# One layer of a hybrid encoder on one core: two projection tiles made together, one more set of weight sums made ahead, and the last product order of the last unit

## The chip, the cores and the metric

The kernel runs on one core of one Trainium2 chip. It is a single launch with no host arithmetic. The metric is the device time of the launch in microseconds (us), taken as the median of several runs. Five engines work side by side, each with its own instruction queue that runs in order: PE (matrix products; PEld is its weight load), DVE (elementwise work), ACT (elementwise functions and casts), POOL, and SP, which here does little but issue DMA transfers. An instruction waits at the head of its queue for semaphores, and what stands behind it waits with it.

## The reference, cut to what matters

```python
xn = RMSNorm(x);  y = xn @ W_in                       # 512 tokens x 2048, 59 column tiles of 128
h  = x + concat[GDN(y_gdn), RWKV7(y_rwkv)] @ W_out    # chunked recurrences of 64 tokens
h += CrossAttn(RMSNorm(h), RMSNorm(mem))              # 4 heads into 256 memory tokens (wk: keys)
u  = relu(RMSNorm(h) @ W_up) ** 2                     # 2048 -> 8192
h += u @ W_down                                       # 8192 -> 2048
out = RMSNorm_final(h)
```

All arrays are float32. Products are made from a high and a low part of each weight: `hi` is the weight rounded to the format that PE reads, `lo = w - hi`, and the products with both are added in PSUM.

## The kernel before

**Order of the work.** Every stage is written as Python generators that yield single operations. The planner `run` keeps a clock for each engine and, at each turn, issues the operation that could start first (a rank breaks ties). The result is a fixed order in each engine's queue; the clocks are the planner's own, so an order can be planned for times that the chip then does not keep. Changing one generator therefore also moves instructions of other generators that are in flight at the same time.

**Input projection.** For each of the 59 tiles `py0` to `py58`, two weight halves of 128x1024 are loaded (512 KB each) into a ring of three raw buffers `wraw`. ACT casts `whi<-wraw`, DVE makes `wlo<-wraw,whi`; these pairs form a ring of three as well. `gemm_` then issues three products for each of 16 row blocks (`xhi*whi`, `xlo*whi`, `xhi*wlo`), and DVE evicts the tile (`y<-py,rstd`). `gemm_` can work on several tiles at once: then it takes a half of each and goes through the row blocks once, tile by tile; the first two tiles are made that way. Between these products the recurrences of the heads are fitted in (`pkk`, `ri7x`, `ri7w`, `ri7s`, `ri7t`, `ri7u`, `pov` and so on are small PE products of the last head; `gk`, `k`, `r`, `E` are their operands, made by DVE; POOL makes an inverse that SP carries through DRAM as `bg16T`, `bg16U`). Around the last two tiles the memory tokens are loaded through the same raw ring (`wraw<-in_memT`) and become `mhl0` to `mhl15`, in the space that the blocks of x leave. After the projection come the keys: `kp0`, `kp1` and so on, from halves of `wk`.

**Down.** `u @ W_down` is done with seven products instead of eight for each pair of blocks. A unit of Down, such as (2,1), covers a quarter of the inner dimension (first number, `e`) and one of two column halves (second number, `m`). Its seven products are named B11, B21, T2, T1, T3, B22, T4 and use these weights: B11 takes the block A11, B21 takes A12, T4 takes A22, and the other four take sums of blocks: s1 = A21 + A22, s2 = s1 - A11, s3 = A11 - A21, s4 = A12 - s2. In most units the sums were made ahead: `presum` uses free moments of earlier stages to load columns of the four blocks, make the sums on DVE and store them to DRAM (`Sd`, in the trace `sd_s`). A unit then loads 28 halves of 512 KB, 4 for each product. For (3,0) and (3,1) the list `INSITU` says otherwise: each is split into two units, (3,0,(0,)), (3,0,(1,)), (3,1,(0,)) and (3,1,(1,)), called (3,0,0) to (3,1,1) below, and the sums are made by DVE in the loaded buffers themselves (`insitu`, two halves x of 128x1024 each). Such a unit has 14 halves, loads 8, and one of its products takes half as long as one of a full unit.

Each product writes two PSUM banks, for two blocks of 128 tokens: `mxd`, `mmd`, `mgd` or `scrd`, `scgd`. B11, T2, T3 and T4 share one pair of banks and add up in it, T1 and B22 another; B21 has its own. After each product DVE adds the bank to a row of the result, `h<-h,scrd` (a "snap"), and the next product in the same bank waits for that. The first and second 128 tokens (tokens 0 and 1 below) are complete after T4, tokens 2 and 3 after B22. When all four column blocks of a token block are complete, `final` takes the squares (ACT), and `store` makes the norm, scales by ACT (two column blocks) and DVE (two), and writes out 4 transfers of 256 KB, two from ACT's queue and two from SP's.

**Buffers at the end.** `wfree` holds the raw buffers (6, and 4 more, the tiles `ab` and `ws`, once the activations of Down are all cut), `hfree` the three hi/lo pairs. `loads` takes raw buffers in order; `splits` takes pairs in the order of the products.

Of the kernel before, what the change touches and what calls it, by code (L numbers as in the profile page):

```python
# [17 lines left out]
P = 128  # L18
# [55 lines left out]
def build(tc, I, out):  # L74
# [301 lines left out]
    mem4 = [I["memT"][:, k4 * 4:k4 * 4 + 4, :] for k4 in range(4)]  # L376
    NSQ = (50, 51, 52, 53)
    wq = [("w", I["w_in"][n][:, h * 1024:(h + 1) * 1024]) for h in range(2) for n in range(2)]
    for n in range(2, NIN):
        wq += [("s", mem4[j]) for j in range(4) if n == NSQ[j]]  # L380
        wq += [("w", I["w_in"][n][:, h * 1024:(h + 1) * 1024]) for h in range(2)]
    kpo = [(0, 0), (1, 0), (0, 1), (1, 1)] + [(n, h) for n in range(2, KD) for h in range(2)]
    INSITU = ((3, 0), (3, 1))
    GROUPS = [(e, m) for e in range(8) for m in range(2) if (e // 2, m) not in INSITU]
    A11, A21, A22, A12 = range(4)
    Sd = {(e, m, j): pd.tile([P, 2048], F32, name=f"sd{e}_{m}_{j}", tag=f"sd{e}_{m}_{j}")
          for e, m in GROUPS for j in ("s1", "s2", "s3", "s4")}
# [177 lines left out]
    def projections():  # L565
        pts = [psb(f"py{n}") for n in range(2)]
        yield from gemm_(pts, xhi, xlo, 0)
        for n in range(2):
            chain(evict(n, pts[n]), 0)
        for n in range(2, NIN):  # L570
# [10 lines left out]
            yield from gemm_([pt], xhi, xlo, 2 * n, left="x" if n == NIN - 1 else None)  # L581
            chain(evict(n, pt), 0)
        yield after("py", NIN - 2)
        kpt = {}
        for i, (n, h) in enumerate(kpo):
            if h == 0:
                yield after("kp", n - 2) if n >= 2 else after("py", NIN - 1)
                kpt[n] = psb(f"kp{n}", "mm", 2)
            pt = kpt[n]
            yield half(NKP + i)  # L590
            wh, wl = halves[NKP + i]
            for k in range(8 * h, 8 * h + 8):
                yield lambda: len(mhl) > k
                yield TE.matmul(pt, wh[:, k % 8 * P:k % 8 * P + P], mhl[k], start=k == 0, stop=False)
            for k in range(8 * h, 8 * h + 8):
                yield TE.matmul(pt[:, 0:M], wl[:, k % 8 * P:k % 8 * P + P], mhl[k][:, 0:M], start=False, stop=k == KD - 1)
            used.add(NKP + i)
            if h == 0:
                continue
            t = act_tile(f"khl{n}")  # L600
            khl.append(t)
            chain(kevict(n, pt, t[:, 0:M], t[:, M:2 * M]), 0)
        for i in range(2 * KD):
            n, g = i // 2, i % 2
            if i == 0:
# [1171 lines left out]
    def loads():  # L1777
        for u in units:
            kind, e, m = u[:3]
            if kind == "u":  # L1780
                src = I["w_up"][e]
                for i in (A11, A12, A22, A21) if u == units[0] else (A11, A21, A22, A12):
                    raws[u, i] = r = yield from take(wfree)
                    yield SY.dma_start(r, src[i])
                    events.add(("raw", u, i))
                continue
            if (e, m) in INSITU:
                for ws in (A11,), (A12,), (A21, "s1", A22):
                    for x in xs(u):
                        f, z = 2 * e + x // 2, x % 2  # L1790
                        for w in ws:
                            raws[u, w, x] = r = yield from take(wfree)
                            if w != "s1":
                                yield SY.dma_start(r, I["w_dm"][f, m, w][:, z * 1024:z * 1024 + 1024])
                                events.add(("raw", u, w, x))
                continue
            for i, w in order_of(u):
                for x in range(4):
# [5 lines left out]
                    events.add(("raw", u, i, x))  # L1804

    def ready(*keys):
# [43 lines left out]

    def insitu():
        for u in units:
            if u[0] != "d" or u[1:3] not in INSITU:
                continue
            for x in xs(u):
                yield lambda: all(("raw", u, w, x) in events for w in (A11, A21, A22))
                a11, a21, a22, s1 = (raws[u, w, x] for w in (A11, A21, A22, "s1"))
                yield tt(s1, a21, a22)
                events.add(("sum", u, "s1", x))
                yield tt(a21, a11, a21, ALU.subtract)  # L1860
                events.add(("sum", u, "s3", x))
                yield after("half", u, B11, x)
                yield tt(a11, s1, a11, ALU.subtract)
                events.add(("sum", u, "s2", x))
            for x in xs(u):
                yield after("half", u, B21, x)
                a11, a12 = (raws[u, w, x] for w in (A11, A12))
                yield tt(a12, a12, a11, ALU.subtract)
                events.add(("sum", u, "s4", x))
                yield after("half", u, T2, x)  # L1870
                wfree.append(a11)

    def splits():
        for u in units:
            if u[0] == "d" and u[1:3] in INSITU:
                for i, w in order_of(u):
                    for x in xs(u):
                        yield (after("sum", u, w, x) if isinstance(w, str) else after("raw", u, w, x))
                        r = raws[u, {"s2": A11, "s3": A21, "s4": A12}.get(w, w), x]
# [3 lines left out]
                        if w not in (A11, A12, "s2"):  # L1883
                            wfree.append(r)
                continue
            if u[0] == "d":
                for i, w in order_of(u):
                    for x in range(4):
# [219 lines left out]
    def downout(u, t, tag):  # L2108
# [6 lines left out]

        (x, kx) = banks_of[u, tag, t]
        mul = lambda i: after("mul", u, i, t)
        for i, tg, m, half, end in ((B11, tag, 0, 0, 0), (B21, "mm", 0, 0, 1), (T2, tag, 0, 1, 0), (T1, "mg", 1, 1, 0),
                                    (T3, tag, 1, 1, 0), (B22, "mg", 0, 1, 1), (T4, tag, 1, 0, 1)):
            yield mul(i)  # L2120
            b, kb = banks_of[u, tg, t]
            yield add(m, half, b)
# [136 lines left out]
    def finals():  # L2259
        yield lambda: acts_done and len(abfree) == 8  # L2260
        wfree.extend(abtiles + sfree_)
        yield after("spare7")
        wf.extend((hp[7][:, 0], hp[7][:, 1]))
        for _ in range(2):
# [132 lines left out]
```

## Time and profile before

| | us |
|---|---|
| median of 3 runs | 2909.23 |
| lowest and highest | 2908.71, 2913.34 |
| the profiled execution | 2912.32 |
| its span in the profile | 2910.4 |
| PE busy | 2872.1 |
| PE without work, all together | 38.3 |

The span runs from the first to the last recorded instruction or transfer; 1.9 us of the profiled execution lie outside it. PE is busy for nearly all of the span, so the time that a change can win is in the gaps of PE and at both ends; a row of the waits view gives how long an engine stood and what released it. In a timeline row the columns are start, duration, engine, line, operation, output and inputs, how many are merged in the row, and in brackets the idle time before it. In a row of the windows view stand the stretch, its length, the busy time of each engine, the clock that PE was granted (1.00 is full), the share of the DMA engines in use and what they moved.

### The profile page before, as it was taken

The numbers are of one execution on the slowest core, as the hardware profiler recorded it, in microseconds if no ns is written. First come the engines' busy times: TensorE is split into PE (matmuls) and PEld (weight loads), VectorE is DVE, ScalarE is ACT, GpSimd is POOL, SyncE is SP. The second block draws the span as 40 slices with busy tenths as digits, with TensorE's granted clock in tenths as the row PEclk, the third lists the DMA queues.
The fourth block names the chain that finished last, engine by engine and source line by source line (L and its number), as shares of the span: only waits on it lengthen the run. The fifth ranks groups of instructions, "written<-read, shape, count | busy, mean of one in ns | idle before, by whom it ended". The sixth has DMA issues, their size and how long they took to land.

```text
span 2910.4 us, 49156 instructions
## 1 busy us (share of the span) xinstructions
PE 2872.1 (99%) x18794; PEld 2421.0 (83%) x18794; DVE 2330.0 (80%) x3539; ACT 1569.2 (54%) x2233; POOL 224.8 (8%) x547
## 2 busy tenths in 40 slices
PE   8999999999999999999999999999999999999998
PEld 7887877777877888879988888888888888888786
DVE  7787787787887877769956898899998878776997
ACT  6454555555655555664445556555555644454544
POOL 0213213223213000000000000000000000000000
PEclk9999999999999999999999999999999999999999
DMA  5646656556666788784322354565556878876633
GB/s 190 177 140 181 165 156 171 167 153 180 179 168 188 219 255 274 230 286 152 125 95 88 108 167 156 192 202 193 184 195 193 290 225 283 259 236 207 198 109 105
DMA packets 314300, 541.47 MB, mean 186 GB/s; under 512 B 100360, under 2 KB 185612, under 8 KB 314064
## 3 DMA queue, kind: packets, MB, share of 16 engines
q1 hardware_dynamic: 286672, 506.87, 56.5%
q10 hardware_dynamic: 27392, 31.46, 3.1%
q8 instruction: 147, 2.41, 0.3%
q14 instruction: 89, 0.73, 0.1%
HBM read 436.11 MB, written 102.12 MB: 185 GB/s over the span
## 4 chain that ended last, share of the span: by engine, by line
PE 92%; DMA 3%; DVE 2%; ACT 1%; issue 1%; ACTq 0%; SPq 0%; DVEq 0%
PE py L256 22%; PE mxu L256 12%; PE mgu L256 6%; PE mgd L256 6%; PE mxd L256 6%; PE op L122 5%; PE vp L122 3%; PE sc L122 3%; PE at L122 3%; PE kp L256 3%; PE mmu L256 3%; PE scgd L256 3%; PE scrd L256 3%; PE mmd L256 3%; PE kq L256 3%; DMA wraw<-in_wo 1%
## 5 line engine op out<-in xcount | busy, mean ns | idle before, releaser
L256 ACT CAST whi<-wraw 128x1024 fp32r<-128x1024 f32 (+1 forms) x364 | 381.4, 1049 | 395.8 <-PE py L256 148.7
L256 DVE TENSOR_TENSOR wlo<-wraw,whi 128x1024 fp32r<-128x1024 f32 (+1 forms) x364 | 448.3, 1232 | 104.8 <-ACT whi L256 96.5
L256 PE MATMUL py<-xhi,whi 128*128 128x512 f32 x928 | 372.3, 401 | 7.9 <-ACT xhi L256 7.9
L256 PE MATMUL py<-xlo,whi 128*128 128x512 f32 x928 | 373.8, 403 | 0.0
L256 PE MATMUL py<-xhi,wlo 128*128 128x512 f32 x928 | 373.1, 402 | 0.0
L256 ACT CAST whi<-w 128x1024 fp32r<-128x1024 f32 x181 | 190.4, 1053 | 221.4 <-PE mxu L256 48.3
L256 DVE TENSOR_TENSOR wlo<-w,whi 128x1024 fp32r<-128x1024 f32 x181 | 220.9, 1222 | 54.1 <-ACT whi L256 52.0
L256 PE MATMUL mxu<-cb,whi 128*128 128x512 f32 x1016 | 255.0, 393 | 0.0
L256 PEld LDWEIGHTS py<-xhi,whi 128*128 128x128 f32 x928 | 175.1, 189 | 42.0 <-ACT xhi L256 7.9
L256 PEld LDWEIGHTS mxu<-cb,whi 128*128 128x128 f32 x1016 | 182.9, 189 | 32.6
L256 PEld LDWEIGHTS py<-xhi,wlo 128*128 128x128 f32 x928 | 175.2, 189 | 35.2 <-issue 1.8
L256 PEld LDWEIGHTS py<-xlo,whi 128*128 128x128 f32 x928 | 175.1, 189 | 35.1 <-DVE xlo L256 0.5
L131 DVE TENSOR_TENSOR wlo<-wraw,whi 128x1024 fp32r<-128x1024 f32 x112 | 136.8, 1223 | 44.9 <-ACT whi L130 44.0
L130 ACT CAST whi<-wraw 128x1024 fp32r<-128x1024 f32 x112 | 117.6, 1051 | 85.2 <-PE op L122 30.4
L256 PEld LDWEIGHTS mxu<-cb,wlo 128*128 128x128 f32 x1016 | 138.7, 190 | 10.5 <-DVE wlo L256 0.7
L256 PE MATMUL mxu<-cb,wlo 128*128 128x256 f32 x1016 | 142.3, 283 | 0.3 <-DVE wlo L256 0.3
L256 ACT ACT_TABLE_LOAD x87 | 111.6, 1283 | 36.7 <-DVE suml_gn L256 15.8
L256 PE MATMUL mgu<-cb,whi 128*128 128x512 f32 x512 | 129.5, 394 | 1.3 <-ACT whi L256 1.2
L256 PE MATMUL mxd<-whi,cb 128*128 128x512 f32 x512 | 127.0, 390 | 2.7 <-ACT whi L256 2.7
L256 PE MATMUL mgd<-whi,cb 128*128 128x512 f32 x512 | 126.5, 389 | 0.0
L122 PE MATMUL op<-ob,whi 128*128 128x256 f32 (+1 forms) x752 | 115.3, 304 | 0.2 <-ACT whi L130 0.2
L256 PEld LDWEIGHTS mxd<-whi,cb 128*128 128x128 f32 x512 | 95.9, 188 | 23.6 <-ACT whi L256 3.5
(943 smaller groups left out, 6432.6 us busy)
## 6 DMA issues: line engine op xcount, KB each, us to landing
wraw<-in_w_in SPq DMA_DIRECT2D x116, 512.0 KB, 4.4
wraw<-in_w_up SPq DMA_DIRECT2D x65, 512.0 KB, 3.8
w<-in_w_up SPq DMA_DIRECT2D x63, 512.0 KB, 3.8
ds<-in_w_dm SPq DMA_DIRECT2D x128, 205.0 KB, 4.1
sd_s<-ds SPq DMA_DIRECT2D x128, 205.0 KB, 5.1
w<-sd_s SPq DMA_DIRECT2D x48, 512.0 KB, 4.8
wraw<-sd_s SPq DMA_DIRECT2D x48, 512.0 KB, 4.8
wraw<-in_w_dm SPq DMA_DIRECT2D x46, 512.0 KB, 5.0
```

The lines of the kernel that those rows point to most:

```text
L122: PE.matmul(o, l, r, start=start, stop=stop, skip_group_check=again)
L130: S.copy(hi, src)
L131: V.tensor_tensor(out=lo, in0=src, in1=hi.bitcast(F32), op=ALU.subtract)
L256: f(*a, **k)
```

## The change

Four places change.

1. `projections` and the load list `wq`: the tiles py57 and py58 are made together by one call of `gemm_`. Their four weight halves are loaded in the order first half of 57, first of 58, second of 57, second of 58.
2. `PRE`: the group of (3,0,0) is added to the groups whose sums are made ahead. `presum` gets 2048 columns more to do, and the unit loads 14 halves and makes no sums itself.
3. In the last unit, (3,1,1), the products come in the order B11, T2, T1, T3, B22, B21, T4. Its s4 goes into A11's buffer, because A12 is now needed after it.
4. `more`: when all loads have been issued, free `ab` and `ws` buffers become hi/lo pairs as well.

```diff
-    for n in range(2, NIN):
+    for n in range(2, NIN - 2):
         wq += [("s", mem4[j]) for j in range(4) if n == NSQ[j]]
         wq += [("w", I["w_in"][n][:, h * 1024:(h + 1) * 1024]) for h in range(2)]
+    wq += [("w", I["w_in"][n][:, h * 1024:(h + 1) * 1024]) for h in range(2) for n in (NIN - 2, NIN - 1)]
...
-    GROUPS = [(e, m) for e in range(8) for m in range(2) if (e // 2, m) not in INSITU]
+    PRE = ((3, 0, 0),)
+    GROUPS = [(e, m) for e in range(8) for m in range(2) if (e // 2, m) not in INSITU or (e // 2, m, e % 2) in PRE]
...
+            if n == NIN - 2:
+                yield after("py", n - 1)
+                pts = [psb(f"py{n + i}", "mm", 2) for i in range(2)]
+                yield from gemm_(pts, xhi, xlo, 2 * n, left="x")
+                for i in range(2):
+                    chain(evict(n + i, pts[i]), 0)
+                continue
...
-            if (e, m) in INSITU:
-                for ws in (A11,), (A12,), (A21, "s1", A22):
+            if (e, m) in INSITU and u[1:] not in PRE:
+                for ws in ((A11,), (A21, "s1", A22), (A12,)) if u == units[-1] else ((A11,), (A12,), (A21, "s1", A22)):
...
+    def more(tag, olds):
+        yield after("loaded")
+        yield lambda: all(any(x is o for x in wfree) for o in olds)
+        wfree[:] = [x for x in wfree if not any(x is o for o in olds)]
+        pair = []
+        for i, o in enumerate(olds):
+            x = pu.tile([P, 1024], F32R, tag=tag, name=f"{tag}r{i}", bufs=2)
+            slot[x.tensor.name], holder[o.tensor.name] = o.tensor.name, x.tensor.name
+            pair.append(x)
+        hfree.append(pair)
...
+        if u == units[-1]:
+            return (B11, A11), (T2, "s2"), (T1, "s1"), (T3, "s3"), (B22, "s4"), (B21, A12), (T4, A22)
         return (B11, A11), (B21, A12), (T2, "s2"), (T1, "s1"), (T3, "s3"), (B22, "s4"), (T4, A22)
...
-                yield after("half", u, B21, x)
+                yield after("half", u, T2, x)
+                yield lambda: ("raw", u, A12, x) in events
                 a11, a12 = (raws[u, w, x] for w in (A11, A12))
-                yield tt(a12, a12, a11, ALU.subtract)
+                if u == units[-1]:
+                    yield tt(a11, a12, a11, ALU.subtract)
+                else:
+                    yield tt(a12, a12, a11, ALU.subtract)
+                    wfree.append(a11)
                 events.add(("sum", u, "s4", x))
-                yield after("half", u, T2, x)
-                wfree.append(a11)
```

What the engines' queues hold at the places that the prediction speaks of follows, before and after. PE has the same number of rows in both.

**End of the projection, DVE.** `gk` is an operand of the head's product `pkk`; `mhl12` to `mhl15` come from the last load of memory tokens; `wlo_117` belongs to the first half of the keys. Before:

```order
L256 TENSOR_TENSOR y1_179<-py58_10355,rstd_120 128x512
L256 SCALAR_TENSOR_TENSOR mhl10_10485<-wraw125_10219,prm_72,mhl10_10485 128x256
L256 SCALAR_TENSOR_TENSOR mhl11_10489<-wraw125_10219,prm_72,mhl11_10489 128x256
L256 TENSOR_TENSOR gk_569_10477<-gkn_567_10456,gqd_553_10172 128x512
L256 TENSOR_TENSOR wlo_117_10497<-wraw126_10405,whi_117_10496 128x1024
L256 SCALAR_TENSOR_TENSOR mhl12_10511<-wraw127_10442,prm_72,mhl12_10511 128x256
L256 SCALAR_TENSOR_TENSOR mhl13_10514<-wraw127_10442,prm_72,mhl13_10514 128x256
```

The same place after the change:

```order
L256 SCALAR_TENSOR_TENSOR mhl12_10517<-wraw127_10450,prm_72,mhl12_10517 128x256
L256 SCALAR_TENSOR_TENSOR mhl13_10520<-wraw127_10450,prm_72,mhl13_10520 128x256
L256 SCALAR_TENSOR_TENSOR mhl14_10526<-wraw127_10450,prm_72,mhl14_10526 128x256
L256 SCALAR_TENSOR_TENSOR mhl15_10532<-wraw127_10450,prm_72,mhl15_10532 128x256
L256 TENSOR_TENSOR gk_569_10470<-gkn_567_10452,gqd_553_10176 128x512
L256 TENSOR_TENSOR wlo_118_10538<-wraw128_10494,whi_118_10537 128x1024
L256 TENSOR_TENSOR gEs_560_10320<-pkk7_10541,gEs_560_10320 128x512
```

`gk` has moved from ahead of `mhl12` to behind `mhl15`. On PE the product `pkk`, which stood ahead of `kp0`, now stands behind the first half of `kp0`, and a half of `kp1` now stands between `ri7w` and `ri7s`.

**Start of unit (3,0,0), DVE.** `rstd`, `spare` and `h0` are rows of the result; `wraw`, `ws`, `ab`, `w` with no `whi` among the inputs are sums made in place. Before:

```order
L256 TENSOR_TENSOR rstd_120<-rstd_120,mxd3_0_0_0_26448 128x512
L256 TENSOR_TENSOR spare_17936<-spare_17936,mxd3_0_0_1_26449 128x512
L256 TENSOR_TENSOR wraw273_17932<-wraw271_17930,ab0_17939 128x1024
L256 TENSOR_TENSOR wraw271_17930<-wraw272_17931,wraw271_17930 128x1024
L256 TENSOR_TENSOR wraw272_17931<-wraw273_17932,wraw272_17931 128x1024
L256 TENSOR_TENSOR ws0_17937<-ab1_17940,ws1_17938 128x1024
L256 TENSOR_TENSOR rstd_120<-rstd_120,mmd3_0_6_0_26494 128x512
L256 TENSOR_TENSOR spare_17936<-spare_17936,mmd3_0_6_1_26495 128x512
L256 TENSOR_TENSOR wlo_261_17942<-wraw272_17931,whi_261_17941 128x1024
L256 TENSOR_TENSOR ab1_17940<-w20_17933,ab1_17940 128x1024
```

After:

```order
L256 TENSOR_TENSOR rstd_120<-rstd_120,mxd3_0_0_0_26502 128x512
L256 TENSOR_TENSOR spare_17928<-spare_17928,mxd3_0_0_1_26503 128x512
L256 TENSOR_TENSOR wlo_261_17934<-wraw271_17922,whi_261_17933 128x1024
L256 SCALAR_TENSOR_TENSOR c53_17945<-rcol_16374 128x1
L256 TENSOR_TENSOR wlo_262_17936<-wraw273_17924,whi_262_17935 128x1024
L256 TENSOR_TENSOR rstd_120<-rstd_120,mmd3_0_6_0_26550 128x512
L256 TENSOR_TENSOR spare_17928<-spare_17928,mmd3_0_6_1_26551 128x512
L256 TENSOR_TENSOR wlo_263_17938<-wraw272_17923,whi_263_17937 128x1024
```

Between the two snaps stood four sums and now stand two splits. On SP the 16 stores of the new group stand among the loads of units (1,1) to (2,1); the last of them, `sd6_0_s4<-acc2`, stands directly ahead of the second A12 half of (3,0,0).

**Start of the last unit, DVE.** The rows around the first snap, `h3<-h3,scrd`. Before:

```order
L256 TENSOR_TENSOR h5_12815<-h5_12815,mxd3_1_0_1_26938 128x512
L256 TENSOR_TENSOR wlo_262_17944<-w21_17934,whi_262_17943 128x1024
L256 TENSOR_TENSOR wraw273_17932<-ab0_17939,ws1_17938 128x1024
L256 TENSOR_TENSOR wlo_263_17946<-wraw271_17930,whi_263_17945 128x1024
L256 TENSOR_TENSOR h3_12813<-h3_12813,scrd3_1_0_0_27173 128x512
L256 TENSOR_TENSOR h3_12813<-h3_12813,scgd3_1_0_1_27174 128x512
```

After:

```order
L256 TENSOR_TENSOR h5_12807<-h5_12807,mxd3_1_0_1_26988 128x512
L256 TENSOR_TENSOR wlo_262_17936<-wraw271_17922,whi_262_17935 128x1024
L256 TENSOR_TENSOR ab0_17931<-w20_17925,ws1_17930 128x1024
L256 TENSOR_TENSOR w20_17925<-ws0_17929,w20_17925 128x1024
L256 TENSOR_TENSOR ws0_17929<-ab0_17931,ws0_17929 128x1024
L256 TENSOR_TENSOR h3_12805<-h3_12805,scrd3_1_0_0_27222 128x512
L256 TENSOR_TENSOR h3_12805<-h3_12805,scgd3_1_0_1_27223 128x512
```

Four instructions of 128x1024 now stand between `h5` and `h3` instead of three, and the product behind B11 is T2, in the same bank, instead of B21.

More of the change, by code (lines that the diff above doesn't have):

```diff
@@ L569, in projections @@
             chain(evict(n, pts[n]), 0)
-        for n in range(2, NIN):
+        for n in range(2, NIN - 1):
             if n == NSQ[3] + 3:
@@ L579, in projections @@
                 yield after("py", n - 2)
+            if n == NIN - 2:
[5 more added lines that the diff above has]
+                continue
             pt = psb(f"py{n}", "mm", 2)
-            yield from gemm_([pt], xhi, xlo, 2 * n, left="x" if n == NIN - 1 else None)
+            yield from gemm_([pt], xhi, xlo, 2 * n)
             chain(evict(n, pt), 0)
@@ L1797, in loads @@
             for i, w in order_of(u):
-                for x in range(4):
+                for x in xs(u):
                     f, z = 2 * e + x // 2, x % 2
@@ L1804, in loads @@
                     events.add(("raw", u, i, x))
+        events.add(("loaded",))
+    def more(tag, olds):
[8 more added lines that the diff above has]
+        hfree.append(pair)
     def ready(*keys):
@@ L1852, in insitu @@
         for u in units:
-            if u[0] != "d" or u[1:3] not in INSITU:
+            if u[0] != "d" or u[1:3] not in INSITU or u[1:] in PRE:
                 continue
@@ L1865, in insitu @@
             for x in xs(u):
-                yield after("half", u, B21, x)
+                yield after("half", u, T2, x)
+                yield lambda: ("raw", u, A12, x) in events
                 a11, a12 = (raws[u, w, x] for w in (A11, A12))
-                yield tt(a12, a12, a11, ALU.subtract)
+                if u == units[-1]:
[3 more added lines that the diff above has]
+                    wfree.append(a11)
                 events.add(("sum", u, "s4", x))
-                yield after("half", u, T2, x)
-                wfree.append(a11)
     def splits():
         for u in units:
-            if u[0] == "d" and u[1:3] in INSITU:
+            if u[0] == "d" and u[1:3] in INSITU and u[1:] not in PRE:
                 for i, w in order_of(u):
@@ L1878, in splits @@
                         yield (after("sum", u, w, x) if isinstance(w, str) else after("raw", u, w, x))
-                        r = raws[u, {"s2": A11, "s3": A21, "s4": A12}.get(w, w), x]
+                        r = raws[u, {"s2": A11, "s3": A21, "s4": A11 if u == units[-1] else A12}.get(w, w), x]
                         halves[u, i, x] = hl = yield from take(hfree)
@@ L1882, in splits @@
                         events.add(("half", u, i, x))
-                        if w not in (A11, A12, "s2"):
+                        if w not in (A11, "s2") and (w != A12 or u == units[-1]):
                             wfree.append(r)
@@ L1887, in splits @@
                 for i, w in order_of(u):
-                    for x in range(4):
+                    for x in xs(u):
                         yield after("raw", u, i, x)
@@ L2117, in downout @@
         mul = lambda i: after("mul", u, i, t)
-        for i, tg, m, half, end in ((B11, tag, 0, 0, 0), (B21, "mm", 0, 0, 1), (T2, tag, 0, 1, 0), (T1, "mg", 1, 1, 0),
-                                    (T3, tag, 1, 1, 0), (B22, "mg", 0, 1, 1), (T4, tag, 1, 0, 1)):
+        outs = {B11: (tag, 0, 0, 0), B21: ("mm", 0, 0, 1), T2: (tag, 0, 1, 0), T1: ("mg", 1, 1, 0),
+                T3: (tag, 1, 1, 0), B22: ("mg", 0, 1, 1), T4: (tag, 1, 0, 1)}
+        for i, _ in order_of(u):
+            tg, m, half, end = outs[i]
             yield mul(i)
@@ L2261, in finals @@
         wfree.extend(abtiles + sfree_)
+        chain(more("ab", abtiles), 0.5)
+        chain(more("ws", sfree_), 0.5)
         yield after("spare7")
```

## The prediction

> **What bounds the kernel now.** I read the engine totals first, then the chain that ended last, then PE's waits.
>
> ```profile
> span 2910.4 us, 49156 instructions
> PE 2872.1 (99%) x18794; PEld 2421.0 (83%) x18794; DVE 2330.0 (80%) x3539; ACT 1569.2 (54%) x2233; POOL 224.8 (8%) x547
> PE 92%; DMA 3%; DVE 2%; ACT 1%; issue 1%; ACTq 0%; SPq 0%; DVEq 0%
> PE py L256 <- ACT xhi L256: 7.9, 1, 7.9
> PE mxd L256 <- ACT whi L256: 2.7, 2, 2.4
> PE kp L256 <- ACT whi L256: 2.2, 1, 2.2
> PE pkk L256 <- DVE gk L256: 2.2, 1, 2.2
> PE ri7u L256 <- DVE k L256: 1.5, 1, 1.5
> ```
>
> PE is the bound, and the change leaves its products as they are. So only its idle 2910.4 - 2872.1 = 38.3 us can be won: the start, a few single waits, and the end after the last product. Three of the waits stand at the end of the projection (`kp`, `pkk`, `ri7u`), one at the start of Down's unit (3,0,0) (`mxd`). I take the four places in order of time.
>
> **A, the joint tiles and the step to the keys.**
>
> ```profile
> L256 DVE TENSOR_TENSOR wlo<-wraw,whi 128x1024 fp32r<-128x1024 f32 (+1 forms) x364 | 448.3, 1232 | 104.8 <-ACT whi L256 96.5
> 930.00:933.00 3.00, 1.53 (x66) 1.19 (x65) 2.89 (x6) 1.35 (x3) 1.90 (x5) 1.00 0.45 147
> 933.00:937.00 4.00, 4.00 (x21) 3.19 (x15) 3.29 (x5) 1.65 (x5) 3.45 (x8) 0.57 0.63 182
> 914.56 1.16 PE L256 MATMUL pkk<-gk,gkn 128*128 128x128 f32 x8 [2.17 <-DVE gk L256]
> 915.47 2.08 PE L256 MATMUL kp<-mhl,whi 128*128 128x512 f32 x8
> 921.57 1.88 PE L256 MATMUL kp<-mhl,whi 128*128 128x512 f32 x7 [2.25 <-ACT whi L256]
> 908.80 0.61 SPq L256 DMA_DIRECT2D wraw<-in_wk  x1
> 913.46 1.04 ACT L256 CAST whi<-wraw 128x1024 fp32r<-128x1024 f32 x1
> 918.67 1.71 ACT L256 ACTIVATE mhl<-wraw,prm 128x256 fp32r<-128x256 f32 x4 [4.17 <-DMA wraw<-in_memT]
> 919.21 1.68 DVE L256 SCALAR_TENSOR_TENSOR mhl<-wraw,prm,mhl 128x256 fp32r<-128x256 f32 x4 [3.46 <-ACT mhl L256]
> 901.04 0.69 DVE L256 TENSOR_TENSOR y<-py,rstd 128x512 f32<-128x512 f32 x1 [0.49 <-PE py L256]
> 912.42 0.69 DVE L256 TENSOR_TENSOR y<-py,rstd 128x512 f32<-128x512 f32 x1 [0.96 <-PE py L256]
> ```
>
> The last two tiles end 11.38 us apart for 48 products, at most 0.24 each. In the joint run the fourth half needs the pair that py57's first half leaves, and six products (1.4 us) stand between; its cast (1.04, as at 913.46) and its split (1.23, the group's mean) take 2.3. That is a new stall of 0.9: the projection ends near 913.3. The freed x blocks bring nothing here: the first load of `wk` is issued at 908.80 from the same place in SP's row, behind the transfers that wait for POOL, and its cast ends at 914.5. `kp0` starts there, 0.9 earlier than now, because `pkk` no longer stands ahead. The idle time up to it is 0.9 + 1.2 against 2.17: no difference. `kp0`'s first half (3.3 us) ends at 917.8. Then `pkk` waits for `gk`, which DVE now has behind `mhl12` to `mhl15`, and these wait for the memory load that ACT shows at 918.67: `gk` ends at 921.6, PE stands 3.8 us where it stood 2.25. Behind it `kp1` now fills the time in which DVE makes `k`, so the 1.5 us before `ri7u` shrink to about 0.2. Sum of A: 0.0 + 1.55 - 1.3 = +0.3. Nearest row for the low end: all three waits gone but `pkk`'s, -1.7; for the high end: `ri7u`'s wait stays, +1.8.
>
> The clock adds an uncertainty: after the stretch with 1.53 of 3 us busy PE was granted 0.57 for 4 us, which costs 1.7. I take the same loss on both sides, since a gap of that kind stays; it could go (-1.7) or come twice (+1.7).
>
> The Trainium skill (TensorE: Matmul & The Clock Gate, "What's actually happening") says that the clock halves after a window of about 3.4 us that was idle, free-running, and comes back after a busy one. The trace here has 0.57 after a stretch that was half busy, so the rule's condition is too narrow for this case, and its two levels fit. By the rule the present kernel would lose nothing here and a gap of 3.8 us could hold a whole idle window: +1.7 on A.
>
> **B, unit (3,0,0).**
>
> ```profile
> 2740.53 1.98 PE L256 MATMUL mxd<-whi,cb 128*128 128x512 f32 x8
> 2745.97 1.98 PE L256 MATMUL mmd<-whi,cb 128*128 128x512 f32 x8
> 2761.01 1.99 PE L256 MATMUL mgd<-whi,cb 128*128 128x512 f32 x8
> 2746.91 1.22 DVE L256 TENSOR_TENSOR wraw<-wraw,ab 128x1024 f32<-128x1024 f32 x1
> 2757.57 1.22 DVE L256 TENSOR_TENSOR w<-w,w 128x1024 f32<-128x1024 f32 x1
> 2740.50:2761.00 20.50, 17.50 (x73) 13.21 (x72) 19.49 (x25) 8.43 (x10) 0.00 (x0) 1.00 0.23 80
> ```
>
> B11, B21 and T2 take 5.44 each (2745.97 - 2740.53), so T1 would start at 2740.53 + 16.32 = 2756.85; it starts at 2761.01. The 4.16 us between are DVE: eight sums of 1.22 from 2746.91 to 2758.8 stand among the splits, and DVE is busy 19.49 of 20.50. With the sums read from DRAM they are gone, and so is the stall: -4.2. What is late next is the loads, 14 instead of 8: they are issued some 10 us before their use. I take the range -4.4 to -2.0, half of it if the loads come late.
>
> **D, the sums made ahead.** Sixteen loads and 16 stores of 256 KB and 16 sums of 128x512 more between 2500 and 2735.
>
> ```profile
> 2436.00:2512.00 76.00, 76.00 (x337) 62.97 (x336) 53.03 (x60) 29.85 (x30) 0.00 (x0) 1.00 0.91 299
> 2588.00:2664.00 76.00, 76.00 (x337) 62.97 (x336) 43.84 (x44) 29.83 (x30) 0.00 (x0) 1.00 0.63 206
> 2664.00:2740.00 76.00, 76.00 (x337) 62.97 (x336) 67.02 (x84) 43.57 (x56) 0.00 (x0) 1.00 0.75 241
> 2731.84 0.33 SPq L256 DMA_DIRECT2D wraw<-in_w_dm  x1
> 2723.83 0.70 DVE L256 TENSOR_TENSOR ab<-ws,ab 128x512 f32<-128x512 f32 x1
> ```
>
> 8.4 MB over the last 152 us add 55 GB/s to 206 and 241, which comes to what the first row carries (299 GB/s) with PE at 76.00 of 76.00. DVE takes 16 x 0.7 = 11 us into 152 - 111 = 41 us of free time. So 0. The last store waits on SP for a sum that stands two rows behind `ab<-ws,ab` (2723.83), that is about 2725, and the loads behind it come in time: the row of 2731.84 is one of them today. Range 0 to +2 (a load of 5 us landing late once).
>
> **C, the last unit and the end.**
>
> ```profile
> 2864.38 1.98 PE L256 MATMUL mmd<-whi,cb 128*128 128x512 f32 x8
> 2858.88 1.28 DVE L256 TENSOR_TENSOR h<-h,mxd 128x512 f32<-128x512 f32 x2
> 2864.13 0.69 DVE L256 TENSOR_TENSOR h<-h,scrd 128x512 f32<-128x512 f32 x1 [0.56 <-PE scrd L256]
> 2896.57 0.61 PE L256 MATMUL scgd<-wlo,cb 128*128 128x512 f32 x2
> 2897.17 8.27 SPq L256 DMA_DIRECT2D out_dram<-h  x8
> 2897.80 0.67 DVE L256 TENSOR_TENSOR h<-h,scgd 128x512 f32<-128x512 f32 x1
> 2900.87 2.74 DVE L256 SCALAR_TENSOR_TENSOR h<-h,r,sl 128x512 f32<-128x512 f32 x4
> out_dram<-h SPq DMA_DIRECT2D x8, 256.0 KB, 4.0
> 2897.20:2910.40 13.20, 0.00 (x0) 0.00 (x0) 5.56 (x11) 4.66 (x9) 0.00 (x0) 0.58 0.84 299
> ```
>
> At the front of the unit T2 now follows B11 in the same bank. DVE has from 2858.88 the two adds (1.2), a split and three sums (1.22 each, starting 1.14 apart, 4.6) ahead of the snap: it starts near 2864.6 instead of 2864.13, and with 0.7 for its length T2 starts near 2865.3 instead of 2864.38: a stall of 1.0. Bounds: 0.45 (the snap without the queue) and 2.1 (one more sum late).
>
> At the end, PE finishes at 2897.18, and 13.2 us follow. All 16 transfers of 256 KB (4.2 MB) leave in them or just before; SP's eight issues end at 2905.44, 4.96 before the span's end. After the change tokens 2 and 3 are complete after B22, two products or 10.9 us ahead of PE's end, so their 8 transfers are under way by then. What remains behind PE's end is the chain of tokens 0 and 1. Today its add starts at 2897.80, 0.6 behind PE, after scalings of token 2, and its last scaling ends at 2900.87 + 2.74 = 2903.61, with two scalings of token 3 in the same row. Take 0.4 for the add and half of 2.74 off: the last scaling ends near 2901.8, and its issue, which today comes 1.8 behind it because earlier ones are queued (8 in 8.27 us), follows in 0.4: 2902.2, which is 3.2 earlier. With the same 4.96 behind it: -3.2. Bounds: 0, if writing is the limit anyway, and -5.
>
> The Trainium skill (DMA: Bandwidth & Descriptors, "Anatomy of one DMA") gives a transfer about 2 us plus its bytes at 436 GB/s, estimated 2.6 for 256 KB, against 4.0 measured here with the queues full. By the page the tail would come out 1.4 shorter still, and the sum at -7.5.
>
> **The sum.** +0.3 - 4.2 + 0 + 1.0 - 3.2 = -6.1. The profiled execution took 2912.32, 1.9 outside the span; it stands 3.1 above the median. Against itself the changed kernel would take 2906.2; against the median 2909.23 it is 2903.1.
>
> **The rivals.** (1) The end does not shorten. For it speaks that the scalings of tokens 2 and 3 by DVE stand behind B21's adds in its queue, so half of their transfers start only in the last product; against it, that the other half goes from ACT earlier. Then only the 1.0 stall is left of C: +0.3 - 4.2 + 1.0 = -2.9, 2906.3. (2) The step to the keys costs more: the low clock comes twice and `ri7u` keeps its wait, +3.2 more on A: -2.9, 2906.3 as well. That the joint run frees x early and yet does not start the keys earlier belongs here; the change would then not do there what it does on paper. (3) Slower: SP's queue holds the loads of (3,0,0) behind the last store. DVE makes its sum among the activations of the last quarter; its loads must land first, under a DMA share near 0.9. Up to about 2737 the halves behind it land before their split (2731.84 plus 5); each us more is a us of PE. It decides above 2743, and gives with a sum at 2750: -6.1 + 13 = +6.9, 2916. Against it: the other groups made in the same way at 2436 to 2512 cost PE nothing. (4) Better: the low clock goes as well and the tail follows the shorter landing: -6.1 - 1.7 - 1.4 = -9.2, 2900.0.
>
> **How the numbers follow.** 0.2% of this time is 5.8 us, about what a measurement can tell from no change; faster is below 2903.4, slower above 2915.1. The forecast sits close to that line, so the chances split there. I give the forecast (2901 to 2905) 0.52, of which 0.4 lies on the faster side; rival (4) 0.12; rivals (1) and (2) 0.26 together, both within the bound; rival (3) 0.10, slower or nearly. Faster 0.52, within 0.2% 0.39, slower 0.09. The range goes from rival (4) with 0.5 to spare, 2899.5, to 2911.1, where A, B, the stall and the tail all stand at their poor ends (+1.8 - 2.0 + 2.1 + 0 = +1.9); past it lies rival (3).
>
> **What would show it.** Right: no wait of PE between 2740 and 2762, T1 of (3,0,0) 16.3 us behind B11; one gap of 3 to 4 us ahead of `pkk`, none of over 0.5 at `ri7u`; a wait of about 1 us at the second `scrd` of the last unit; the span's end some 10 us behind PE's. Wrong: waits of PE on a `whi` behind an `sd_s` load, a clock below 1.00 over more than 4 us after 912, or half of the outputs issued behind PE's end.

## The result

| | before | after |
|---|---|---|
| median of 13 runs each, us | 2910.98 | 2906.89 |
| lowest and highest | 2906.44, 2919.24 | 2901.03, 2910.92 |
| profiled execution | 2912.32 | 2905.73 |
| its span | 2910.4 | 2903.3 |

The ratio of after to before is 0.9982 with a 95% interval of 0.9974 to 0.9990, that is 5.2 us less (2.9 to 7.6). The changed kernel is faster, and by a little less than the 0.2% that were called the limit of what can be told. The predicted change of -6.1 lies in the interval and the time in the range; the predicted 2903.1 stands 3.8 below the median, of which 1.75 is that the kernel before took 2910.98 over 13 runs where the three runs at hand gave 2909.23.

The waits of PE in the profile after (total, times, longest), longest first:

```profile
PE py L256 <- ACT xhi L256: 6.8, 1, 6.8
PE pkk L256 <- DVE gk L256: 4.0, 1, 4.0
...
PE pvr L256 <- DVE suml_pvr L256: 1.5, 1, 1.5
...
PE kp L256 <- ACT whi L256: 1.3, 1, 1.3
PE kq L256 <- DVE y L256: 1.2, 1, 1.2
PE scrd L256 <- DVE h L256: 1.0, 1, 1.0
```

The row of `mxd` (2.7) is gone, and so is that of `ri7u`. `pkk` has grown from 2.2 to 4.0. New are `scrd` and two small waits of the joint tiles (`py`, 0.5 and 0.2), which were predicted, and `pvr`, which was not.

**The step to the keys.** Timeline of after, PE, the end of the projection and what follows; then the windows view of the same place:

```profile
902.14 0.50 PE L256 MATMUL py<-xhi,wlo 128*128 128x512 f32 x1 [0.45 <-DVE wlo L256]
913.92 2.14 PE L256 MATMUL kp<-mhl,whi 128*128 128x512 f32 x8 [1.26 <-ACT whi L256]
920.99 2.08 PE L256 MATMUL pkk<-gk,gkn 128*128 128x128 f32 x8 [3.99 <-DVE gk L256]
924.06 3.06 PE L256 MATMUL kp<-mhl,whi 128*128 128x512 f32 x8
989.97 0.47 PE L256 MATMUL pvr<-suml_pvr,bonesr 128*128 128x512 f32 x1 [1.53 <-DVE suml_pvr L256]
```

```profile
916.00:920.00 4.00, 1.00 (x9) 0.79 (x7) 1.34 (x4) 1.70 (x4) 0.00 (x0) 0.92 0.93 354
920.00:924.00 4.00, 3.01 (x40) 2.73 (x40) 2.99 (x5) 2.71 (x3) 0.00 (x0) 0.50 0.64 187
```

The joint tiles stall for 0.45 at the last halves, `kp0` starts 1.1 earlier than it did (913.92 against 915.47, less 0.41 for the earlier start of the program), and PE then stands 3.99 at `pkk`. Within that gap the granted clock falls to 0.50 and it stays there behind it (from 919.33 to 926.16 in the trace's record of the clock): eight `kp` products take 3.06 where they took 2.14 ten microseconds earlier. To see what the whole step costs, take one product of `py` well ahead of it and the first `vp` behind it, before and after:

```profile
782.92 0.50 PE L256 MATMUL py<-xlo,whi 128*128 128x512 f32 x1
1126.67 2.11 PE L122 MATMUL vp<-mhl,whi 128*128 128x512 f32 x8 [0.95 <-DVE y L256]
```

```profile
782.51 0.50 PE L256 MATMUL py<-xlo,whi 128*128 128x512 f32 x1
1126.90 2.12 PE L122 MATMUL vp<-mhl,whi 128*128 128x512 f32 x8 [0.21 <-DVE y L256]
```

That is 343.75 before and 344.39 after: +0.64 (predicted +0.3).

**Unit (3,0,0).** After, PE, the first halves of its B11 and of T1, and the stretch ahead of it:

```profile
2740.13 1.98 PE L256 MATMUL mxd<-whi,cb 128*128 128x512 f32 x8
2756.45 1.98 PE L256 MATMUL mgd<-whi,cb 128*128 128x512 f32 x8
```

```profile
2500.00:2740.00 240.00, 240.00 (x1061) 198.72 (x1060) 197.15 (x240) 122.46 (x144) 0.00 (x0) 1.00 0.84 271
```

T1 starts 16.32 behind B11, where it was 20.48: -4.16, and no PE row between them has a wait. The profile of `e2_pre` below has the same 16.32. In the 240 us ahead of it, in which the 16 sums are made, PE is busy all the time.

**The last unit and the end.** After, PE at T2 and at the very end; DVE and the two queues that issue the outputs; the landing of SP's outputs; the windows of the end:

```profile
2860.93 1.16 PE L256 MATMUL scrd<-whi,cb 128*128 128x512 f32 x4 [0.97 <-DVE h L256]
2893.23 0.61 PE L256 MATMUL scgd<-wlo,cb 128*128 128x512 f32 x2
2893.88 0.69 DVE L256 TENSOR_TENSOR h<-h,scgd 128x512 f32<-128x512 f32 x1 [0.58 <-PE scgd L256]
2889.96 8.58 SPq L256 DMA_DIRECT2D out_dram<-h  x8
2898.68 0.34 ACTq L256 DMA_DIRECT2D out_dram<-h  x1
out_dram<-h SPq DMA_DIRECT2D x8, 256.0 KB, 2.9
```

```profile
2885.00:2890.00 5.00, 5.00 (x24) 4.14 (x23) 2.85 (x9) 3.17 (x6) 0.00 (x0) 1.00 0.32 122
2890.00:2895.00 5.00, 3.84 (x17) 2.83 (x16) 3.96 (x8) 3.54 (x10) 0.00 (x0) 1.00 0.98 296
```

The stall at T2 is 0.97, and the unit takes 39.47 instead of 38.23, +1.24 with the slower products behind the stall. PE ends at 2893.84 and the span 9.46 later instead of 13.2: -3.76. Transfers run from 2887 on, under the last products, and 8 of the 16 outputs are issued before PE ends. Before, 2 of the 16 were and a third as PE ended, and next to nothing moved in that stretch. The same windows of before:

```profile
2885.00:2890.00 5.00, 5.00 (x24) 4.13 (x23) 4.74 (x8) 3.45 (x6) 0.00 (x0) 1.00 0.00 0
2890.00:2895.00 5.00, 5.00 (x24) 4.14 (x23) 3.02 (x8) 2.30 (x8) 0.00 (x0) 1.00 0.01 2
```

The two profiles account for the whole difference of the spans: -0.41 up to `py` at 782 (the first product starts at 6.8 instead of 7.9, which varies from execution to execution between 6.3 and 8.2, whatever the kernel), +0.64, -0.63 between `vp` and (3,0,0), -4.16, +1.24, -3.76, together -7.1. Without the two stretches that the change doesn't touch it is -6.0.

### The profile page after: what moved, and what is told of

It is laid out like the page before. It is cut to its first block, busy times and chain, and to the rows that moved or that the text cites. A ratio compares the mean times of both kernels' runs of the same rounds, so it can differ in the third digit from the quotient of the medians.

```text
span 2903.3 us, 49235 instructions
## 1 busy us (share of the span) xinstructions
PE 2871.2 (99%) x18794; PEld 2420.5 (83%) x18794; DVE 2332.9 (80%) x3547; ACT 1570.7 (54%) x2233; POOL 226.2 (8%) x547
## 4 chain that ended last, share of the span: by engine, by line
PE 93%; DMA 2%; DVE 2%; ACT 1%; issue 1%; ACTq 0%; SPq 0%; DVEq 0%
PE py L256 22%; PE mxu L256 12%; PE mgu L256 6%; PE mgd L256 6%; PE mxd L256 6%; PE op L122 6%; PE vp L122 3%; PE sc L122 3%; PE at L122 3%; PE mmd L256 3%; PE mmu L256 3%; PE kp L256 3%; PE scrd L256 3%; PE scgd L256 3%; PE kq L256 3%; PE vo L122 1%
## 5 line engine op out<-in xcount | busy, mean ns | idle before, releaser
L256 DVE TENSOR_TENSOR wlo<-w,whi 128x1024 fp32r<-128x1024 f32 x176 | 214.8, 1221 | 50.1 <-ACT whi L256 46.8
L256 ACT CAST whi<-ws 128x1024 fp32r<-128x1024 f32 x75 | 78.9, 1052 | 75.3 <-PE mgu L256 49.1
```

The costliest lines, as they stand in the source:

```text
L256: f(*a, **k)
```

## The experiments

Each group of runs stands beside runs of the kernel before on the same chip, and the ratios are to those.

**One part alone.** `e1_joint` is the kernel before with only the joint tiles; `e2_pre` with only the third unit's sums made ahead; `e3_last` with only the last unit's order and `more`. `e4_nojoint` is the changed kernel without the joint tiles.

```diff
 # e1_joint, against before
+    wq += [("w", I["w_in"][n][:, h * 1024:(h + 1) * 1024]) for h in range(2) for n in (NIN - 2, NIN - 1)]
...
+                yield from gemm_(pts, xhi, xlo, 2 * n, left="x")
 # e2_pre, against before
+    PRE = ((3, 0, 0),)
 # e3_last, against the changed kernel: the projection as before, and
-    PRE = ((3, 0, 0),)
+    PRE = ()
 # e4_nojoint, against the changed kernel: the projection as before
```

> Only the joint projection tiles. The theory that sums the places (A +0.6, B -4.2, sums ahead 0, stall in the last unit +1.0, end -3.7 us) expects +0.6 us (ratio 1.0002), with a wait of PE of about 4 us ahead of the head's product pkk and the start of the values vp about 0.6 us later against the last tiles before py57. The rival, that the joint run frees x earlier and lets the keys start earlier, expects vp earlier by 1 us or more and a ratio of 0.9997 or less.

> Only the sums of unit (3,0,0) made ahead. The theory expects -4.2 us (ratio 0.9986): no wait of PE between B11 and T1 of that unit, T1 starting 16.3 us behind B11 where it was 20.5, and no new wait in units (1,1) to (2,1), which carry the new transfers. The rival, that these transfers cost PE something, expects waits on a whi there and -2 to -3 us (0.9990 to 0.9993).

> Only the last unit's order, with the buffers turned into hi/lo pairs. The theory expects +1.0 for the wait of the second product and -3.7 at the end, some +0.2 for small waits: -2.5 us (ratio 0.9991), the span ending 9.5 us behind PE where it was 13.2. The rival, that writing 4.2 MB sets the end, expects 12 to 13 us behind PE and +0 to +1 us in all.

> The changed kernel with the projection tiles as before. The theory expects -6.7 us against before (ratio 0.9977), 0.6 us less than the changed kernel, with PE's waits at pkk, kp and ri7u as before. The rival, that the joint tiles gain, expects 0.9984 or more.

| kernel | ratio to before | 95% interval | in us |
|---|---|---|---|
| e1_joint | 1.0007 | 0.9999 to 1.0016 | +2.0 |
| e2_pre | 0.9981 | 0.9973 to 0.9990 | -5.5 |
| e3_last | 0.9996 | 0.9987 to 1.0005 | -1.2 |
| sum of the three | | | -4.7 |
| the change | 0.9982 | 0.9974 to 0.9990 | -5.2 |
| e4_nojoint | 0.9979 | 0.9970 to 0.9988 | -6.1 |

The parts add up to the whole within their intervals, which are some 2.5 us to each side. By these ratios the joint tiles cost time rather than give it, the sums made ahead bring more than their 4.2, and the last unit brings less than its 2.2; but the intervals hold all three predicted values, so the profiles have to say more. For the last unit they bear the forecast out: in `e3_last` PE waits 0.97 at T2 and the span ends 9.7 behind PE. In `e4_nojoint` PE stands 2.2 at `pkk`, as before, and 1.2 at `kp`.

For the joint tiles they do, because ten kernels share the stretch from `py` at 782 to the first `vp`. The six with separate tiles took 343.75, 342.93, 343.45, 341.42, 341.13 and 340.70 in it, 342.2 in the mean. The four with joint tiles and `gk` behind the memory blocks (after, e1, e5, e6) took 344.39, 344.54, 343.10 and 344.08, 344.0 in the mean. So the term is +1.8; the two groups overlap a little, and the spread within them leaves it uncertain by some 1.4 to each side (an estimate). The profile on which the prediction rested was the slowest of its kind. In all four `pvr` waits 1.2 to 1.5, in none of the six. The sizes fit: in this stretch PE stands idle for 9.2 in the mean of the four and 8.1 in the mean of the six, so `pvr` is more than the whole difference, and the products that run at half clock take 4.8 against 3.1, which makes 0.9 more.

For the sums made ahead the profiles show a second loss at the stall that is taken away. `e3_last` and `e7_traffic` (below) still have it, with the same wait as before. Timeline of `e3_last`, PE, and its windows; then `e7_traffic`, PE:

```profile
2758.40 3.78 PE L256 MATMUL mxd<-whi,cb 128*128 128x512 f32 x8 [2.35 <-ACT whi L256]
2758.40:2762.00 3.60, 3.60 (x9) 2.86 (x10) 2.34 (x2) 1.84 (x2) 0.00 (x0) 0.50 0.53 157
```

```profile
2752.60 2.99 PE L256 MATMUL mxd<-whi,cb 128*128 128x512 f32 x8 [2.33 <-ACT whi L256]
```

```profile
2757.72 2.11 PE L256 MATMUL mxd<-whi,cb 128*128 128x512 f32 x8 [2.36 <-ACT whi L256]
```

The last row is the kernel before. The same eight products behind the same wait take 2.11, 2.99 or 3.78, because in two of the four executions that have this stall the clock goes to half behind it. From the first half of B11 to the second of T1 it was 23.21 in before and in e1, 24.41 in e7 and 25.61 in e3, 24.1 in the mean, against 19.04 without the stall. The term is -5.1 rather than -4.2, since what goes with the stall is also the risk of the slow clock.

**What the sums made ahead cost.** `e7_traffic` is the kernel before that makes and stores the sums of (3,0,0) ahead and does not use them.

```diff
 # against before
-    GROUPS = [(e, m) for e in range(8) for m in range(2) if (e // 2, m) not in INSITU]
+    PRE = ((3, 0, 0),)
+    GROUPS = [(e, m) for e in range(8) for m in range(2) if (e // 2, m) not in INSITU or (e // 2, m, e % 2) in PRE]
```

> The kernel before, which also makes the sums of (3,0,0) ahead and stores them, but does not use them: the unit still makes its own in place. This is the price of the sums ahead alone. The theory expects 0 (ratio 1.0000, within 0.0004) and the 4.2 us of waits at (3,0,0) unchanged; the rival expects +1 to +2 us and waits of PE in units (1,1) to (2,1).

Measured: 0.9999 (0.9990 to 1.0007). The windows view of `e7_traffic` over the stretch in which the sums are made:

```profile
2500.00:2740.00 240.00, 240.00 (x1061) 198.80 (x1060) 195.62 (x240) 123.91 (x146) 0.00 (x0) 1.00 0.80 263
```

DVE has 240 instructions there and 220 in the kernel before, the transfers 263 GB/s and 230; PE is busy for 240.00 of 240.00 in both. The extra work is covered; the interval alone would allow a cost of 2 us.

**What the early outputs are worth.** `e6_hold` is the changed kernel in which the norms of tokens 2 and 3 wait for the last product.

```diff
 # e6_hold, against the changed kernel
+        if t > 1:
+            yield after("mul", units[-1], T4, 1)
         yield DV.tensor_reduce(out=a, in_=cols5[t], axis=AX.X, op=ALU.add)
```

> The changed kernel, but the norms and outputs of tokens 2 and 3 are held until the last product T4 is made, so that all 16 transfers leave at the end again. If the end is shorter because half of the outputs leave under the last two products, it is 12 to 14 us behind PE again: 3 to 4 us more than the changed kernel (ratio 0.9995). If it is shorter because DVE and ACT have less queued for tokens 0 and 1 in this order, the end stays 9.5 to 11 us behind PE.

Measured: 1.0004 (0.9996 to 1.0013), 6.4 us above the changed kernel's ratio. Timeline and windows of `e6_hold`:

```profile
2893.19 0.61 PE L256 MATMUL scgd<-wlo,cb 128*128 128x512 f32 x2
2903.37 0.47 ACTq L256 DMA_DIRECT2D out_dram<-h  x1
2900.00:2905.00 5.00, 0.00 (x0) 0.00 (x0) 0.84 (x2) 2.16 (x3) 0.00 (x0) 0.50 1.06 357
```

PE's products end where they do in the changed kernel, the span ends 15.3 behind them instead of 9.5, and the last output is issued 4.7 later (2903.37 against 2898.68). So what the order of the products buys is that half of the scalings and transfers lie under PE. The expectation had 12 to 14; that it is worse than before (13.2) fits the outputs of token 2 that the kernel before already issues from 2894.52 on, ahead of PE's end, where `e6_hold` issues none.

**The stall at T2.** `e5_alt` is the changed kernel with products that alternate between the two pairs of banks in the last unit.

```diff
 # e5_alt, against the changed kernel
-            return (B11, A11), (T2, "s2"), (T1, "s1"), (T3, "s3"), (B22, "s4"), (B21, A12), (T4, A22)
+            return (B11, A11), (T1, "s1"), (T2, "s2"), (B22, "s4"), (T3, "s3"), (B21, A12), (T4, A22)
```

> The changed kernel with the last unit's products in the order B11, T1, T2, B22, T3, B21, T4, so that no two neighbours share a bank. If the wait of 1 us behind B11 is the shared bank (the next product waits for the add), it is gone: 1.0 to 1.2 us less than the changed kernel (ratio 0.9978), the last unit taking 38.1 us from its first to its last product where the changed kernel took 39.5. If it is DVE's queue alone (three sums ahead of the splits), a wait of about 1 us stays, now on a wlo or whi of T1 or T2.

Measured: 0.9985 (0.9976 to 0.9993), no gain against 0.9982. The wait is gone and the unit takes 38.23 again. But the span now ends 10.55 behind PE instead of 9.46. Timeline of `e5_alt`, PE and DVE at the end:

```profile
2890.34 0.61 PE L256 MATMUL scgd<-wlo,cb 128*128 128x512 f32 x2
2891.16 0.73 DVE L256 SCALAR_TENSOR_TENSOR h<-h,r,sl 128x512 f32<-128x512 f32 x1
2891.81 0.68 DVE L256 TENSOR_TENSOR h<-h,scgd 128x512 f32<-128x512 f32 x1
```

In the changed kernel the add behind the last product starts 0.04 behind PE's end (2893.88); here it starts 0.86 behind it (2890.95), because scalings of an earlier token still stand ahead of it on DVE. So the stall at T2 costs PE 1.24, and by the spans of the profiles the kernel 0.2 to 0.6 (0.2 here, 0.5 from `e8_gk` to `e9_gkalt` and 0.6 from `e4_nojoint` to `e10_nojalt` below), since without it the end behind PE is 0.7 to 1.1 longer. The ratios can't tell that from nothing.

**`gk` ahead of the last memory blocks.** In the changed kernel `gk` stands on DVE behind `mhl15`. `e8_gk` lets the last memory block wait for it; `e9_gkalt` adds the order of e5; `e10_nojalt` has the order of e5 and separate tiles.

```diff
 # e8_gk, against the changed kernel
         yield DV.tensor_tensor(out=kb, in0=kn, in1=B, op=ALU.mult)
+        events.add(("kb", h))
...
     def memory(k4, raw):
+        if k4 == 3:
+            yield after("kb", 7)
```

> The changed kernel, but the last load of memory tokens is split only after DVE's gk has been put in its queue, so gk stands ahead of mhl12 to mhl15 again. If the 4 us ahead of pkk come from that place in DVE's queue, they are gone; next late is the whi of kp1's first half, a wait of 2 to 3 us as before, and with pkk and the ri7 products done in it the step to the keys is 1.5 to 2.5 us shorter (ratio 0.9976). If gk is late for another reason, the wait ahead of pkk stays at 3 us or more and the time is the changed kernel's.

> The changed kernel with both of its new stalls taken out: gk ahead of the last memory loads (as in e8_gk) and the last unit in the order B11, T1, T2, B22, T3, B21, T4 (as in e5_alt). If the stall at pkk and the stall at the last unit's T2 are separate losses on PE, the gains add: e8_gk ended 6.9 us below the kernel before, less another 1.0 for T2 makes 7.9, ratio 0.9973, with the last unit at 38.2 instead of 39.5 and no wait of PE on h. Rival: T2's stall is made good behind PE's end (the outputs were waiting for DMA anyway), and the ratio stays at e8_gk's 0.9974 or goes up, with the span's end over 10 us behind PE's.

> The changed kernel without the joint tiles and with the last unit in the order of e5_alt. If the joint tiles are worth nothing once gk is ahead, this comes out as e9_gkalt within 1.5 us (0.9975); PE stands about 2.2 at pkk and 2.2 at kp as before. Rival: the joint tiles free the x blocks early and win 1 us or more where gk does not stand in the way, so e9_gkalt is ahead by over 1.5 us.

| kernel | ratio to before | 95% interval | `py` at 782 to `vp` | end behind PE |
|---|---|---|---|---|
| e8_gk | 0.9974 | 0.9965 to 0.9984 | 342.40 | 9.4 |
| e9_gkalt | 0.9977 | 0.9968 to 0.9986 | 341.56 | 10.2 |
| e10_nojalt | 0.9973 | 0.9964 to 0.9983 | 340.70 | 10.2 |

Timeline of `e8_gk`, DVE and PE:

```profile
915.97 0.68 DVE L256 TENSOR_TENSOR gk<-gkn,gqd 128x512 f32<-128x512 f32 x1
917.52 1.05 PE L256 MATMUL pkk<-gk,gkn 128*128 128x128 f32 x8
922.68 2.08 PE L256 MATMUL kp<-mhl,whi 128*128 128x512 f32 x5 [3.87 <-ACT whi L256]
```

`gk` is made at 915.97 instead of 920.25 and `pkk` does not wait, nor does `pvr` later. What is late then is the next half of `wk`: PE stands 3.87 at `kp`, where 2 to 3 had been expected, and the clock falls as it did. The stretch to `vp` takes 342.4 and 341.6, as with separate tiles (342.2), and the ratio goes from 0.9982 to 0.9974, with overlapping intervals. The gain that e9 should have had over e8 (no stall at T2) does not come, as in e5: the rival that was written down for it holds. And e10 is no slower than e9: the joint tiles bring nothing even when `gk` is out of the way. e8 and e10 have the lowest ratios of the study, though their intervals overlap with that of the changed kernel.

## Why the prediction held, and where it was off

| term | predicted | the two profiles | from the means of all profiles with and without it |
|---|---|---|---|
| A, joint tiles and step to the keys | +0.3 | +0.64 | +1.8 |
| B, (3,0,0) | -4.2 | -4.16 | -5.1 |
| D, sums made ahead | 0 | 0 | 0 |
| C, stall at T2 | +1.0 | +1.24 (wait 0.97) | +1.24 |
| C, end | -3.2 | -3.76 | -3.6 |
| sum | -6.1 | -6.0 | -5.7 |

The sum came out, and the wait at T2 (to 0.03), the stall of (3,0,0) in the two profiles (to 0.04) and D, where nothing was late, came out by their own reasons. That the sum did is in part luck: A cost 1.5 more than was said, B and the end gave 0.9 and 0.4 more, and these offset each other. The absolute time, 2906.89, lies outside the 2901 to 2905 of the forecast and is nearer to the 2906.3 of rivals (1) and (2), in part because the kernel before came out 1.75 higher as well.

**A** was too low by 1.5. Its mechanism held step by step up to `ri7u`: a stall in the joint run (0.45 and 0.2 where 0.9 was said), `kp0` earlier, 3.99 at `pkk` (3.8 said), no wait at `ri7u`. Two steps failed, which the accounting above puts at 1.4 and 0.9; what is left of A is then some -0.4 where +0.3 was said. One was that the chain ended with `ri7u`: `pkk` starts later, so the head's sums are later, and `pvr` waits 1.2 to 1.5 for `suml_pvr` some 70 us on, a product that I had not followed. The other was "the same loss on both sides" for the clock: with the gap of 3.8 to 4.1 the low clock came in four profiles of four, and among the six with separate tiles it stayed away between 900 and 950 in e2 and e7. The prediction had named this sign itself: "a clock below 1.00 over more than 4 us after 912" is among what would show it wrong, and in the changed kernel it is 6.83. Rival (2) named this place and the clock, and priced A at +3.5 with a wait of `ri7u` that did not come. The bound of +1.8 for "`ri7u`'s wait stays" holds the value, by another wait; by the prediction's own terms, with nothing taken off for `ri7u`, that bound is +1.55, and its -1.7 can't be worked out from the rows that it shows.

**B** was taken from one execution in which the stall passed without a slow clock. Of the three others with this stall one passed in the same way, and two cost 1.2 and 2.4 more.

The **end** came 0.5 better. The sum had the end of the last issue at PE's end + 5.0 and 4.96 behind it; it came at + 5.2 (2899.02) with 4.3 to the span's end. Rival (1), that the end doesn't shorten, is out by the 9.46 itself, and `e6_hold` shows why: it is 15.3 when the outputs are held. That "half of the outputs issued behind PE's end" would show the prediction wrong was drawn too wide: 8 of 16 are, but they are the 8 of tokens 0 and 1, which the prediction's own sum leaves there. The Trainium skill (DMA: Bandwidth & Descriptors, "Anatomy of one DMA") has, for a transfer issued from POOL, about 2 us plus its bytes at 436 GB/s, which is an estimate of 2.6 for 256 KB. The outputs here are issued from SP and ACT, and no run shows that price for them: SP's landed in 2.9 in the median and in 4.0 before, ACT's in 3.5 and in 3.4 before. Behind the last issue 0.7 was won, not 1.4.

Rival (3), loads of (3,0,0) held behind the last store, did not occur: no wait of PE between 2740 and 2762. Rival (4) needed the slow clock to go; with the gap at `pkk` it stayed. Nearest to its 2900.0 come `e8_gk`, `e9_gkalt` and `e10_nojalt`, with medians of 2902.2, 2902.3 and 2902.0.

Of the chances, 0.52 went to "faster by over 0.2%" and 0.39 to "within 0.2%"; the ratio is -0.18%, so it was the second, though the interval reaches to both sides of the limit. For a forecast of -0.21% the first was a little too much.

## What to carry to other kernels

A step that is moved behind a load in one queue delays everything that its result feeds: follow that chain to its last product (here `gk`, `pkk`, `pvr`, 70 us apart), not only to the next wait. A stall of the bounding engine is to be priced from several executions, since what it costs beyond its length changes from one to the next: here one and the same stall cost 4.2, 4.2, 5.4 and 6.6. And before a stall near the end is taken out, see whether the engine that finishes behind it has the time: here the last add then stood behind scalings on DVE, and 1.24 us on PE were worth 0.2 to 0.6.

## What the runs showed of the hardware

The granted clock behind one and the same stall differs between executions of the same instructions. `pkk` with separate tiles, in `e2_pre`, and in `e4_nojoint`:

```profile
912.01 1.16 PE L256 MATMUL pkk<-gk,gkn 128*128 128x128 f32 x8 [2.17 <-DVE gk L256]
```

```profile
914.85 2.07 PE L256 MATMUL pkk<-gk,gkn 128*128 128x128 f32 x8 [2.18 <-DVE gk L256]
916.58 2.77 PE L256 MATMUL kp<-mhl,whi 128*128 128x512 f32 x8
```

Over the profiles here, gaps of PE of about 2.2 to 2.5 us (at `pkk`, `kp` and `mxd`) were followed by the slow clock in 4 cases of 13, and those of 3.3 to 4.1 us in 7 of 7. The loss was 1.2 to 2.4 us each where it could be measured. The Trainium skill (TensorE: Matmul & The Clock Gate, "What's actually happening") has a free-running window of about 3.4 us that must be idle for the clock to halve. That the window runs free agrees with the traces, as the next paragraph shows. That it must be idle from end to end does not: here 2.18 was enough, and in the kernel before even the 1.47 at `ri7u` (the 0.57 that the prediction shows), and the runs decide.

The record of the clock in the traces says when it comes. Ahead of PE's end each piece of low clock lasts 3.41 or 6.83 us, and in the two executions that have two pieces these start a whole number of steps of 3.413 us apart (538 in `e3_last`, 398 in `e6_hold`). So the clock of an execution changes on a grid of such steps, and it goes with how long PE stands within one of them. Over the twelve profiles, once the products have begun, a step at full clock with 1.9 us or more of idle PE was followed by a slow one in 9 of 9 cases, one with 1.45 to 1.9 in 5 of 21, and one with 0.9 to 1.45 in none of 40. Where the gap falls on the grid differs between executions, and that is why the same wait is cheap in one and dear in another. The gap of 2.17 at `pkk` lies within one step in `e10_nojalt`; in before a step ends in it, and 1.68 is left for the next. The windows of `e10_nojalt`, then of before:

```profile
912.33:915.74 3.41, 1.24 (x8) 0.78 (x8) 2.68 (x5) 1.35 (x2) 0.00 (x0) 1.00 0.91 185
915.74:919.15 3.41, 3.41 (x13) 2.83 (x12) 0.63 (x1) 0.02 (x1) 0.00 (x0) 0.50 0.87 251
```

```profile
912.88:916.29 3.41, 1.73 (x12) 1.60 (x13) 2.85 (x5) 1.35 (x2) 0.00 (x0) 1.00 0.66 122
916.29:919.70 3.41, 3.04 (x46) 2.42 (x44) 0.49 (x2) 1.03 (x3) 0.00 (x0) 1.00 0.95 339
```

A gap of 3.8 or more leaves at least 1.9 in one step wherever it falls, which fits the slow clock behind every one of them. So one profile can't price a shorter gap. The clock is a likely source of the spread between runs of one kernel (9.9 us over 13 runs of the changed one), but no run here isolates it.
